# Dilated attention outputs read back into two tiles, and both branches combined behind the fourth and fifth token tile of the next head pair's projection

## The chip, the cores and the metric

One core of one Trainium2 chip runs one program that computes the whole reference. The metric is the time of one execution on the device in microseconds (us); less is better. TensorE (PE in the rows; PEld is its weight load) multiplies matrices, VectorE (DVE), ScalarE (ACT) and GpSimd (POOL) do the element-wise work, and SP issues the DMA transfers. Each engine runs its own queue in order.

## The reference, cut to what matters

A decoder trunk of two layers (an even and an odd one) over 1024 tokens of width 1024, all in float32. The change lies in the even layer's mixer, in the mixture of dilated attention branches with 8 heads of 64. Branches of the same head are joined by a softmax over their log-denominators:

```python
B_BRANCHES = ((128, 1), (512, 4), (2048, 16))

def even_mixer(h, w_in, ...):
    ...
    qh = rms_norm(heads(q), q_g)
    kh = rms_norm(heads(k), k_g)
    vh = heads(vb)
    outs, lses = [], []
    for window, dilation in B_BRANCHES:
        o_r, l_r = dilated_branch(qh, kh, vh, window, dilation)
        outs.append(o_r)
        lses.append(l_r)
    wts = jax.nn.softmax(jnp.stack(lses), axis=0)
    o = jnp.einsum('rbhs,rbhsc->bhsc', wts, jnp.stack(outs))
    ...
    return jnp.concatenate([a_out, b_out], axis=-1) @ w_out
```

The even mixer's other half is a gated MLP over chunks (gMLP), the odd layer is gated linear attention, and each layer ends in a gated feed-forward block.

## The kernel before

The eight heads are worked on in four pairs (`PAIRS`). For each pair p:

- `project(p)` (from line 640) takes the 1024 tokens in eight tiles of 128. For each tile n it does 24 matmuls into `pj` (line 185, called from line 651): queries, keys and values of the pair, against eight cast weight tiles `wq`. Then come the norms of queries and keys (ScalarE line 656, VectorE line 658, GpSimd lines 135 and 136, VectorE line 660, GpSimd line 662), the value tile `vN` (ScalarE line 664; it also frees the `pj` bank), the turned queries and keys (`qT` line 678, `kT` line 682), and one attention step `unit` for the branch of dilation 1.
- `unit` (line 614) makes, for each of two heads, scores on TensorE (line 600), a masked minimum on VectorE (line 605), an exponential on ScalarE (line 607 or 609), a turn on TensorE (line 625), a copy `pT` (line 630 on VectorE for even i, line 628 on ScalarE for odd i) and the product with the values into `po` (line 633). Minima and denominators go into columns 128 to 131 of a tile `ot`, outputs into its first 128.
- `dilated(p)` (line 698) does eight such units for the branches of dilation 4 and 16 at once, in the order of the residues, and stores both halves to device memory, `od`.
- For each half g of the tokens, a tile `on` (one buffer) is read back from `od` in token order (line 744), and `combine(p, g, ...)` (line 715) joins it with the tile `ot` that `project(p)` left: a minimum `cM` (line 720), two subtractions and an exponential `cE` (lines 723 and 724), denominators and a reciprocal `cD` (lines 727 to 729), a factor each (line 730), one multiply on GpSimd and one on VectorE (line 733), the sum (line 735), and a store to `bcat` (line 736).

In the program text the combines of pair p stand between `dilated(p)` and `project(p + 1)`. Behind the fourth pair stand `gmlp`, `u_proj` and the output projection.

Weights are loaded and cast by `load_qkv`: raw tiles of two chunks, each chunk cast into two parts by ScalarE (line 100) and VectorE (line 101). The pool of cast weights holds eight tiles, as many as one pair needs, so a tile for the next pair becomes free when the last token tile of this pair has used it. There are two `pj` banks.

The order on each engine is not the order of the text. A planner at build time puts ready instructions of earlier text first, by its own estimate of times, and gives out the buffers of a pool; the resulting queues are fixed, and the waits between engines are added. `keep_in_program_order(ins)`, which the change calls, ties `ins` in that plan behind the instruction of its engine that was traced just before it.

Of the kernel before, what the change touches and what calls it, by code (L numbers as in the profile page):

```python
# [8 lines left out]
F32 = mybir.dt.float32  # L9
# [4 lines left out]
ALU = mybir.AluOpType  # L14
# [4 lines left out]
P = 128  # L19
# [22 lines left out]
def f32(ap):  # L42
    return ap.bitcast(F32)
# [6 lines left out]
def rows(t, n):  # L50
    return t[n * P : (n + 1) * P, :]
# [3 lines left out]
def trunk(ctx: ExitStack, tc: tile.TileContext, a, out):  # L55
    nc = tc.nc
    V, A, G, T, Q = nc.vector, nc.scalar, nc.gpsimd, nc.tensor, nc.sync
# [116 lines left out]
    def tok(n, k):  # L174
        return [hq[k % 2][n // 4][:, i, k // 2, (n % 4) * P : (n % 4 + 1) * P] for i in range(2)]

    def mm_tok(ps, lhs, rhs, nk):

        for k in range(nk):
            L, R = lhs(k), rhs(k)  # L180
            for i in range(2):
                for o, sl in ps:
                    for ii, jj in PASSES:
                        if ii == i:
                            T.matmul(o, L[i], R[jj][:, sl], start=(k == 0 and (ii, jj) == PASSES[0]),  # L185
                                     stop=(k == nk - 1 and (ii, jj) == PASSES[-1]))
# [317 lines left out]
    def load_qkv(p):  # L504
        return [w for kp in range(4)
                for w in load_w(a["w_qkv"][p, kp], f"wq{p}{kp}", 384, gains=g0[:, 2 * kp : 2 * kp + 2])]
# [54 lines left out]
    def attention(ps, at, av, pq, pq0, par0, wq0, gm_open):  # L561
# [30 lines left out]
        def by4(t):  # L592

            return t.rearrange("p s (m r) -> p s r m", r=4)
# [42 lines left out]
            return (at.tile([P, 4, 132], F32, tag="ot", name="ot" + name, bufs=5),  # L637
                    ps.tile([P, 4, P], F32, tag="po", name="po" + name))

        def project(p, ws=None):  # L640


            ws = ws or load_qkv(p)
            pool = pq if p % 2 else pq0
            qT = pool.tile([P, 2, S], F32R, tag="qT", bufs=1, name=f"qT{p}")
            kT = pool.tile([P, 4, S], F32R, tag="kT", bufs=1, name=f"kT{p}")
            vd = dram.tile([S, P], F32, name=f"vd{p}")
            vN, os = [], []
            for n in range(NT):
                pj = ps.tile([P, 512], F32, tag="pj", name=f"pj{p}{n}")  # L650
                mm_tok([(pj[:, :384], slice(0, 384))], lambda k: tok(n, k),
                       lambda k: ws[k], KD)
                qn = pq.tile([P, 256], F32, tag="qn", bufs=2, name=f"qn{p}{n}")
                heads = lambda t: t.rearrange("p (h c) -> p h c", c=64)
                rn = r0[:, n : n + 1]
                A.activation(qn, pj[:, :256], AF.Square, scale=rn)
                ssq = small.tile([P, 4], F32, tag="ss4", name=f"ss{p}{n}")
                V.reduce_sum(ssq, heads(qn), axis=AX.X)
                r = inv_rms(ssq, 4, 64, f"rq{p}{n}")
                V.scalar_tensor_tensor(heads(qn), heads(pj[:, :256]), rn, r[:, :, None].to_broadcast([P, 4, 64]),  # L660
                                       op0=ALU.mult, op1=ALU.mult)
                G.tensor_tensor(qn, qn, gqk, op=ALU.mult)
                vN.append(pq.tile([P, P], F32, tag="vN", bufs=3, name=f"vN{p}{n}"))
                A.mul(vN[n], pj[:, 256:384], rn)  # L664
                Q.dma_start(rows(vd, n), vN[n])
                qs = pq.tile([P, 2, P], F32R, tag="qs", bufs=2, name=f"qs{p}{n}")
                ks = pq.tile([P, 4, P], F32R, tag="ks", bufs=2, name=f"ks{p}{n}")
                split([qs[:, :, :64], qs[:, :, 64:]], heads(qn[:, :P]), hi=G.tensor_copy)
                kk = ks.rearrange("p (h i) (x c) -> p h i x c", i=2, x=2)
                split([kk[:, :, i] for i in range(2)], heads(qn[:, P:])[:, :, None, :].to_broadcast([P, 2, 2, 64]),  # L670
                      hi=G.tensor_copy)
                tq = ps.tile([P, 2, P], F32R, tag="tq", name=f"tq{p}{n}")
                for j in range(2):
                    T.transpose(tq[:, j, :], qs[:, j, :], identr)
                qN = pq.tile([P, 2, P], F32R, tag="qN", bufs=2, name=f"qN{p}{n}")
                A.copy(qN, f32(tq))
                four = lambda t: t.rearrange("p s (r m) -> p s r m", r=4)[:, :, :, 32 * n : 32 * n + 32]
                V.tensor_copy(four(qT), by4(f32(tq)))
                tk = ps.tile([P, 4, P], F32R, tag="tq", name=f"tk{p}{n}")
                for j in range(4):  # L680
                    T.transpose(tk[:, j, :], ks[:, j, :], identr)
                (V.tensor_copy if n % 2 else A.copy)(four(kT), by4(f32(tk)))

                if n % 4 == 0:
                    ot, po = outputs(f"{p}n{n}")
                    os.append(ot)
                m0 = max(n - 1, 0)
                unit(p, f"{p}n{n}", n % 4, ot, po, lambda s: qN[:, s, :],
                     lambda s, i: kT[:, 2 * s + i, :].rearrange("p (r m) -> p r m", r=4)[:, :, 32 * m0 : 32 * n + 32],
                     vN[m0 : n + 1], (mband, None), lambda t: t.rearrange("p (m r) -> p r m", r=4))  # L690
                if n % 4 == 3:
                    A.copy(ot[:, :, :P], po)
            v4 = av.tile([P, 4, 2, P], F32, tag="v4", name=f"v4{p}", bufs=1)
            for b in range(2):
                Q.dma_start(v4[:, :, b, :], vd.rearrange("(b m r) c -> b m r c", b=2, r=4)[b])
            return os, qT, kT, v4

        def dilated(p, qT, kT, v4):

            od = dram.tile([S, 132], F32, name=f"od{p}")  # L700
            for g in range(2):
                ot, po = outputs(f"{p}d{g}")
                for i in range(4):
                    r, b = 2 * g + i // 2, i % 2
                    at0 = r * 256
                    unit(p, f"{p}d{g}{i}", i, ot, po, lambda s: qT[:, s, at0 + b * P : at0 + b * P + P],
                         lambda s, part: kT[:, 2 * s + part, at0 : at0 + b * P + P],
                         [v4[:, r, j, :] for j in range(b + 1)], (mboth, count))
                A.copy(ot[:, :, :P], po)
                for b in range(2):  # L710
                    Q.dma_start(od.rearrange("(b m r) c -> b m r c", b=2, r=4)[b][:, 2 * g : 2 * g + 2, :],
                                ot.rearrange("p (r b) c -> p r b c", b=2)[:, :, b, :])
            return od

        def combine(p, g, os):

            nm = [o[:, :, 128:130] for o in os]
            den = [o[:, :, 130:132] for o in os]
            M = small.tile([P, 4, 2], F32, tag="cM", bufs=2, name=f"cM{p}{g}")
            V.tensor_tensor(M, nm[0], nm[1], op=ALU.min)  # L720
            e = small.tile([P, 2, 4, 2], F32, tag="cE", bufs=2, name=f"cE{p}{g}")
            for i in range(2):
                V.tensor_sub(e[:, i], M, nm[i])
            A.activation(e, e, AF.Exp)
            dd = small.tile([P, 2, 4, 2], F32, tag="cD", bufs=2, name=f"cD{p}{g}")
            for i in range(2):
                V.tensor_mul(dd[:, i], e[:, i], den[i])
            V.tensor_add(dd[:, 0], dd[:, 0], dd[:, 1])
            V.reciprocal(dd[:, 1], dd[:, 0])
            V.tensor_tensor(e, e, dd[:, 1:2].to_broadcast([P, 2, 4, 2]), op=ALU.mult)  # L730
            for i, eng in ((0, G), (1, V)):
                ov = os[i][:, :, :P].rearrange("p n (s c) -> p n s c", s=2)
                eng.tensor_tensor(ov, ov, e[:, i, :, :, None].to_broadcast([P, 4, 2, 64]), op=ALU.mult)
            o0, o1 = (o[:, :, :P] for o in os)
            V.tensor_add(o0, o0, o1)
            Q.dma_start(bcat[g].rearrange("(n p) c -> p n c", p=P)[:, :, p * P : p * P + P], o0)

        made = project(0, wq0)
        for p in range(PAIRS):
            os, *qkv = made  # L740
            od = dilated(p, *qkv)
            for g in range(2):
                on = at.tile([P, 4, 132], F32, tag="on", name=f"on{p}{g}", bufs=1)
                Q.dma_start(on, od.rearrange("(n p) c -> p n c", p=P)[:, 4 * g : 4 * g + 4, :])
                combine(p, g, [os[g], on])
            if p + 1 < PAIRS:
                made = project(p + 1)
            if p + 2 == PAIRS:
                par0.close()
                gm = gm_open()  # L750
# [315 lines left out]
```

## Time and profile before

| | us |
|---|---|
| median of 3 runs | 2256.8 |
| lowest and highest | 2255.03 and 2261.63 |
| the profiled execution's own time | 2256.71 |
| its span (first to last instruction) | 2255.0 |
| TensorE busy | 2189.3 |
| VectorE busy | 1483.4 |
| ScalarE busy | 998.6 |
| GpSimd busy | 470.0 |

All rows come from the one profiled execution. Times in them count from the start of its span. A stretch is a window of that time; the granted clock is 1.00 at TensorE's upper level (2.4 GHz) and 0.50 at the lower (1.2 GHz), and a value between is a mean over the stretch. An arrow `<-` in square brackets names what ended the idle time of the engine ahead of the instruction. Buffer numbers are left out of tile names, but a pair's number stays in some: `pT1n` belongs to pair 1 and the branch of dilation 1, `pT1d` to its dilated part.

### The profile page before, as it was taken

How to read it: one execution, taken by the hardware profiler on the slowest of the kernel's cores; microseconds unless marked ns; L12 is line 12 of the kernel's file. 1: busy time of each engine (PE TensorE's matmuls, PEld its weight loads, DVE VectorE, ACT ScalarE, POOL GpSimd, SP SyncE). 2: the span in 40 equal slices, each digit the busy share in tenths (PEclk: the TensorE clock that was granted, in tenths of full speed). 3: DMA queues.
4: the chain of work that ended last, by engine and by line, in shares of the span. 5: the costliest groups of instructions: out<-in, count | busy, mean ns of one | idle time of the engine just before them, and what ended most of it. 6: DMA issues, size and time to landing. Idle time of an engine off the chain costs nothing.

```text
span 2255.0 us, 29873 instructions
## 1 busy us (share of the span) xinstructions
PE 2189.3 (97%) x10800; PEld 1857.6 (82%) x10800; DVE 1483.4 (66%) x2414; ACT 998.6 (44%) x1830; POOL 470.0 (21%) x487
## 2 busy tenths in 40 slices
PE   7989999998999999999999999999999999999999
PEld 7988978787888888878889888877788888888887
DVE  5567655548888888855574444234889898986554
ACT  5445446336544444434453333222644444444443
POOL 3333320000424243200010111000134343420000
PEclk9999999999999999999999999999999999999999
DMA  4122221442444444585562111356254444457555
GB/s 138 47 72 61 62 68 43 126 161 75 155 167 155 160 156 165 179 281 184 205 227 75 52 57 52 108 168 203 75 171 159 157 158 155 157 181 275 197 187 205
DMA packets 139540, 320.22 MB, mean 142 GB/s; under 512 B 15952, under 2 KB 40528, under 8 KB 139392
## 3 DMA queue, kind: packets, MB, share of 16 engines
q1 hardware_dynamic: 139392, 318.31, 42.1%
q8 instruction: 85, 1.39, 0.3%
q14 instruction: 63, 0.52, 0.1%
HBM read 223.29 MB, written 94.96 MB: 141 GB/s over the span
## 4 chain that ended last, share of the span: by engine, by line
PE 85%; DVE 5%; DMA 4%; ACT 3%; issue 1%; POOL 1%; SPq 0%; DVEq 0%; ACTq 0%; POOLq 0%
PE pgB L254 11%; PE puB L254 11%; PE po L185 6%; PE puC L254 5%; PE pgC L254 5%; PE pv L185 5%; PE pdB L361 5%; PE pdC L361 5%; PE pj L185 4%; PE pdO L361 4%; PE pr L185 4%; PE puA L254 3%; PE pgA L254 3%; PE pdP L361 2%; PE pdQ L361 2%; PE pk L197 2%
## 5 line engine op out<-in xcount | busy, mean ns | idle before, releaser
L96 DVE TENSOR_TENSOR da<-ar,da 128x512 fp32r<-128x512 f32 x154 | 106.2, 689 | 156.9 <-ACT da L95 156.8
L95 ACT CAST da<-ar 128x512 fp32r<-128x512 f32 x154 | 95.9, 623 | 211.2 <-PE pdC L361 92.3
L185 PE MATMUL po<-wo,hq 128*128 128x512 f32 x768 | 185.0, 395 | 2.3 <-ACT hq L100 1.3
L185 PEld LDWEIGHTS po<-wo,hq 128*128 128x128 f32 x768 | 141.6, 188 | 31.3 <-ACT hq L100 2.3
L185 PE MATMUL pj<-wq,hq 128*128 128x384 f32 x768 | 156.2, 353 | 3.2 <-ACT vN L664 2.1
L185 PE MATMUL pv<-wv,hq 128*128 128x256 f32 (+2 forms) x960 | 154.6, 315 | 0.3 <-ACT vN L664 0.2
L185 PEld LDWEIGHTS pv<-wv,hq 128*128 128x128 f32 x960 | 135.0, 192 | 9.6 <-ACT vN L664 0.4
L185 PEld LDWEIGHTS pj<-wq,hq 128*128 128x128 f32 x768 | 138.4, 198 | 4.6 <-ACT vN L664 3.2
L361 PE MATMUL pdB<-dw,da 128*128 128x512 f32 x528 | 136.2, 391 | 1.2 <-ACT dw L95 1.2
L361 PE MATMUL pdC<-dw,da 128*128 128x512 f32 x528 | 135.8, 390 | 0.0
L361 PEld LDWEIGHTS pdB<-dw,da 128*128 128x128 f32 x528 | 98.7, 188 | 22.5 <-ACT dw L95 1.6
L361 PEld LDWEIGHTS pdC<-dw,da 128*128 128x128 f32 x528 | 99.0, 188 | 20.5
L225 POOL TENSOR_TENSOR S1g<-rg 128x512 f32<-128x512 f32 x20 | 28.3, 1417 | 417.3 <-DMA wsd<-D 212.5
L96 DVE TENSOR_TENSOR dw<-wr,dw 128x512 fp32r<-128x512 f32 x154 | 105.7, 686 | 10.4 <-ACT dw L95 10.0
L135 POOL TENSOR_SCALAR rn<-ssq 128x1 f32<-128x1 f32 x24 | 9.6, 399 | 452.4 <-ACT h L143 245.8
L361 PE MATMUL pdO<-dw,da 128*128 128x512 f32 x396 | 102.2, 389 | 0.1
L95 ACT CAST dw<-wr 128x512 fp32r<-128x512 f32 x154 | 95.0, 617 | 13.4 <-DMA wr<-in_w_dn 7.3
L185 PE MATMUL pr<-wr,hq 128*128 128x512 f32 x384 | 97.9, 404 | 0.0
L361 PEld LDWEIGHTS pdO<-dw,da 128*128 128x128 f32 x396 | 74.3, 188 | 15.9 <-DVE dw L96 0.6
L185 PEld LDWEIGHTS pr<-wr,hq 128*128 128x128 f32 x384 | 71.2, 188 | 14.5
L283 DVE SCALAR_TENSOR_TENSOR t<-g,cw,t 128x1022 f32<-128x1022 f32 x44 | 76.8, 1744 | 0.1
L282 DVE SCALAR_TENSOR_TENSOR t<-g,cw,t 128x1023 f32<-128x1023 f32 x44 | 62.5, 1420 | 15.5 <-ACT t L281 15.5
(910 smaller groups left out, 5207.2 us busy)
## 6 DMA issues: line engine op xcount, KB each, us to landing
ar<-actd SPq DMA_DIRECT2D x70, 512.0 KB, 3.5
rg<-in_w_gate SPq DMA_DIRECT2D x44, 512.0 KB, 3.5
ru<-in_w_up SPq DMA_DIRECT2D x44, 512.0 KB, 4.5
rd<-in_w_down SPq DMA_DIRECT2D x44, 512.0 KB, 3.6
wsd<-D SPq DMA_DIRECT2D x88, 256.0 KB, 2.2
wr<-wsd SPq DMA_DIRECT2D x40, 512.0 KB, 4.3
actd<-t SPq DMA_DIRECT2D x66, 256.0 KB, 2.1
wr<-in_w_dn SPq DMA_DIRECT2D x30, 512.0 KB, 4.9
```

The lines of the kernel that those rows point to most:

```text
L95: (hi or A.copy)(dst[0], src)
L96: (lo or V.tensor_sub)(dst[1], src, f32(dst[0]))
L135: G.tensor_scalar(r, ssq, 1.0 / n, EPS, op0=ALU.mult, op1=ALU.add)
L185: T.matmul(o, L[i], R[jj][:, sl], start=(k == 0 and (ii, jj) == PASSES[0]), stop=(k == nk - 1 and (ii, jj) == PASSES[-1]))
L197: T.matmul(ps[h], L[i], hq[k % 2][h][:, jj, k // 2, :], start=(k == 0 and (ii, jj) == PASSES[0]), stop=(k == KD - 1 and (ii, jj) == PASSES ...
L225: (G if f else V).tensor_tensor(sums[name], x, y, op=op)
L254: T.matmul(o, L[ii][:, j * P : j * P + P], right[p][:, jj, j, :], skip_group_check=more, start=(not more and j == 0 and (ii, jj) == PASSES ...
L282: V.scalar_tensor_tensor(t[:, 1:], g[:, : S - 1], w(1), t[:, 1:], op0=ALU.mult, op1=ALU.add)
L283: V.scalar_tensor_tensor(t[:, 2:], g[:, : S - 2], w(0), t[:, 2:], op0=ALU.mult, op1=ALU.add)
L361: T.matmul(o, L[ii][:, t * P : t * P + P], R[jj], skip_group_check=more, start=start and not more and (ii, jj) == PASSES[0], stop=stop and ...
```

## The change

`on` gets two buffers, and both loads of a pair are issued behind `dilated(p)`, ahead of either combine. The combines move into `project(p + 1)`: half 0 behind the attention step of token tile 3 (the fourth), half 1 behind that of tile 4 (the fifth). For the last pair, which has no next projection, both follow the loads directly. The first VectorE instruction of a combine (line 720 before) is pinned with `keep_in_program_order`.

```diff
--- before.py
+++ after.py
@@ -637,7 +637,7 @@
             return (at.tile([P, 4, 132], F32, tag="ot", name="ot" + name, bufs=5),
                     ps.tile([P, 4, P], F32, tag="po", name="po" + name))
 
-        def project(p, ws=None):
+        def project(p, ws=None, then=None):
 
 
             ws = ws or load_qkv(p)
@@ -690,6 +690,8 @@
                      vN[m0 : n + 1], (mband, None), lambda t: t.rearrange("p (m r) -> p r m", r=4))
                 if n % 4 == 3:
                     A.copy(ot[:, :, :P], po)
+                if then and n in (3, 4):
+                    then(n - 3)
             v4 = av.tile([P, 4, 2, P], F32, tag="v4", name=f"v4{p}", bufs=1)
             for b in range(2):
                 Q.dma_start(v4[:, :, b, :], vd.rearrange("(b m r) c -> b m r c", b=2, r=4)[b])
@@ -717,7 +719,7 @@
             nm = [o[:, :, 128:130] for o in os]
             den = [o[:, :, 130:132] for o in os]
             M = small.tile([P, 4, 2], F32, tag="cM", bufs=2, name=f"cM{p}{g}")
-            V.tensor_tensor(M, nm[0], nm[1], op=ALU.min)
+            tc.keep_in_program_order(V.tensor_tensor(M, nm[0], nm[1], op=ALU.min))
             e = small.tile([P, 2, 4, 2], F32, tag="cE", bufs=2, name=f"cE{p}{g}")
             for i in range(2):
                 V.tensor_sub(e[:, i], M, nm[i])
@@ -739,12 +741,20 @@
         for p in range(PAIRS):
             os, *qkv = made
             od = dilated(p, *qkv)
+            ons = []
             for g in range(2):
-                on = at.tile([P, 4, 132], F32, tag="on", name=f"on{p}{g}", bufs=1)
+                on = at.tile([P, 4, 132], F32, tag="on", name=f"on{p}{g}", bufs=2)
                 Q.dma_start(on, od.rearrange("(n p) c -> p n c", p=P)[:, 4 * g : 4 * g + 4, :])
-                combine(p, g, [os[g], on])
+                ons.append(on)
+
+            def then(g):
+                combine(p, g, [os[g], ons[g]])
+
             if p + 1 < PAIRS:
-                made = project(p + 1)
+                made = project(p + 1, then=then)
+            else:
+                then(0)
+                then(1)
             if p + 2 == PAIRS:
                 par0.close()
                 gm = gm_open()
```

## Rows read from the trace of the kernel before

**Rows 1.** The page: busy time, share of the span and instructions of TensorE.

```profile
...
PE 2189.3 (97%) x10800; PEld 1857.6 (82%) x10800; DVE 1483.4 (66%) x2414; ACT 998.6 (44%) x1830; POOL 470.0 (21%) x487
...
```

**Rows 2.** Busy time by stretch: length, engines with counts, clock, DMA.

```profile
...
62.60:91.40 28.80, 26.41 (x179) 25.28 (x177) 18.06 (x45) 13.88 (x36) 11.84 (x21) 1.00 0.25 71
130.60:169.50 38.90, 31.83 (x185) 30.20 (x183) 22.54 (x60) 14.28 (x41) 14.74 (x22) 0.87 0.28 79
208.80:246.60 37.80, 32.14 (x181) 30.83 (x180) 22.03 (x59) 14.30 (x40) 13.68 (x21) 0.82 0.32 90
286.60:325.50 38.90, 33.61 (x179) 28.98 (x178) 23.99 (x56) 17.66 (x36) 12.31 (x20) 0.96 0.29 80
...
```

**Rows 3.** Waits of TensorE, 92 to 420 us: who for whom, total, times, longest.

```profile
...
PE po1n L633 <- DVE pT1n L630: 4.1, 1, 4.1
PE po2n L633 <- DVE pT2n L630: 3.8, 1, 3.8
PE po3n L633 <- DVE pT3n L630: 3.8, 1, 3.8
...
PE pj L185 <- ACT vN L664: 2.1, 2, 1.1
...
```

**Rows 4.** Groups of TensorE, first stretch: busy, mean ns, idle before, releaser.

```profile
...
L633 PE MATMUL po0n<-vN,pT0n 128*128 128x64 f32 x32 | 4.2, 274 | 1.2 <-DVE pT0n L630 1.0 <-ACT pT0n L628 0.2
...
```

**Rows 5.** VectorE in order of time, second boundary: start, length, instruction, idle before.

```profile
...
126.02 0.10 DVE L605 DVE_READ_ACCUMULATOR2_ANT ot1n<- 128x1 f32 x1
128.21 0.17 DVE L720 TENSOR_TENSOR cM<-ot0n,on 128x8 f32<-128x8 f32 x1 [2.10 <-DMA on<-od]
...
136.13 0.17 DVE L720 TENSOR_TENSOR cM<-ot0n,on 128x8 f32<-128x8 f32 x1 [3.41 <-DMA on<-od]
...
137.15 0.71 DVE L728 TENSOR_TENSOR cD<-cD 128x8 f32<-128x8 f32 x1
...
139.20 0.63 DVE L605 CUSTOM_DVE_ANT_1 sm1n<-sc1n,mband 128x256 f32<-128x256 f32 x1
...
141.25 0.68 DVE L735 TENSOR_TENSOR ot0n<-ot0n,on 128x512 f32<-128x512 f32 x1
...
145.93 0.68 DVE L630 COPY pT1n<-pP1n 128x512 f32<-128x512 f32 x1
...
```

**Rows 6.** ScalarE in order of time, second boundary.

```profile
...
136.61 0.22 ACT L724 ACTIVATE cE<-cE 128x16 f32<-128x16 f32 x1 [5.24 <-DVE cE L723]
...
141.28 1.11 ACT L100 ACTIVATE wq<-wq20r,g 128x384 fp32r<-128x384 f32 x2
...
```

**Rows 7.** SP's queue in order of time, second boundary.

```profile
...
132.91 0.43 SPq L744 DMA_DIRECT2D on<-od  x1
...
```

**Rows 8.** TensorE in order of time, second boundary.

```profile
...
137.47 3.94 PE L185 MATMUL pj<-wq,hq 128*128 128x384 f32 x21 [1.14 <-ACT vN L664]
...
148.66 5.89 PE L185 MATMUL pj<-wq,hq 128*128 128x384 f32 x20
...
```

**Rows 9.** VectorE in order of time, first stretch.

```profile
...
67.62 0.62 DVE L605 CUSTOM_DVE_ANT_1 sm0n<-sc0n,mband 128x256 f32<-128x256 f32 x1
...
69.85 1.15 DVE L101 SCALAR_TENSOR_TENSOR wq<-wq10r,g,wq 128x384 fp32r<-128x384 f32 x2
...
73.38 0.68 DVE L630 COPY pT0n<-pP0n 128x512 f32<-128x512 f32 x1
...
```

**Rows 10.** GpSimd in order of time, second boundary.

```profile
...
137.11 0.73 POOL L662 TENSOR_TENSOR qn<-qn,gqk 128x256 f32<-128x256 f32 x1 [3.02 <-DVE cD L727]
...
138.64 1.55 POOL L733 TENSOR_TENSOR ot0n<-ot0n,cE 128x512 f32<-128x512 f32 x1
...
```

**Rows 11.** The tile `on`: from the issue of its load to landing.

```profile
...
DMA to landing us min/median/max: 2.9/3.2/4.5
```

**Rows 12.** Busy time by stretch, two more stretches.

```profile
...
146.00:168.00 22.00, 19.50 (x103) 18.57 (x104) 11.29 (x30) 5.09 (x16) 5.80 (x11) 0.77 0.26 72
400.00:417.00 17.00, 16.25 (x72) 13.16 (x71) 9.69 (x30) 8.23 (x10) 3.04 (x2) 1.00 0.20 48
...
```

## The prediction

> **What bounds the kernel now.** The page comes first: TensorE is busy for 97% of the span [rows 1], so a change to the small vector work of the attention can only win where TensorE stands still or runs on its lower clock level. I therefore asked next, stretch by stretch, where that happens, and then what ended each idle time.
>
> The table of stretches [rows 2] carries most of the argument. Each of its four stretches begins in the seventh token tile of one projection and reaches into the third tile of the next (the last one reaches into the gMLP's value projection): the place where one pair's weights run out and the next pair's must be cast. The first one has no combine in it, since no pair has been through its dilated branch yet; the other three each hold both combines of the pair before. Stretches 1 to 3 do nearly the same TensorE work (179, 185 and 181 matmuls), yet the first takes 28.8 us and the others 38.9 and 37.8. TensorE's idle time is span minus busy time: 2.39, 7.07, 5.66 and 5.29 us. The granted clock is 1.00 in the first, 0.87, 0.82 and 0.96 in the others: part of each was at 1.2 instead of 2.4 GHz. So the first stretch is a control made by the kernel itself.
>
> The waits of TensorE [rows 3] name the idle time: once per pair 4.1, 3.8 and 3.8 us for a VectorE copy of `pT` (line 630), and twice about 1 us for ScalarE's `vN`. In the control the same copy costs 1.0 us [rows 4].
>
> Why the copy is late is read from the three queues at the second boundary. Engines run in the order that the planner wrote, so a wait holds all that is queued behind it. VectorE finishes tile 3's scores at 126.1, then waits 2.10 us for the first `on` and begins combine 0 at 128.21. Later it waits 3.41 us for the second `on`, begins combine 1 at 136.13, and only at 139.20 does tile 4's scores (line 605); the `pT` of tile 4 follows at 145.93, behind most of the casts [rows 5]. ScalarE's exponential of combine 1 waits 5.24 us in ScalarE's queue, and its casts (line 100) start at 141.28 [rows 6]. The second `on` can't come earlier: one buffer, so its load is issued at 132.91, after combine 0 [rows 7]. TensorE meanwhile starts the pair's last token tile at 137.47 and the next pair's first at 148.66, 11.2 us apart [rows 8]. In the control tile 4's second score step runs at 67.62, VectorE's casts (line 101) from 69.85 and the `pT` at 73.38, with no wait for a DMA among them [rows 9].
>
> **The change, part by part.** The sum is made against the profiled execution, 2256.71 us (span 2255.0), which is 0.1 us below the median of 2256.8.
>
> *Combine 0 behind the fourth tile.* The pin puts its first instruction behind the VectorE instruction traced just before it: tile 3's second line 605. The trace has it exactly there already, at 128.21 behind the 126.02 one [rows 5]. So I expect no move and no gain: the wait of 2.10 us stays, and TensorE has projection matmuls over it. With both loads issued together, `on` 0 may land later; the landings go from 2.9 to 4.5 us around 3.2 [rows 11], so up to 1.3 us more wait per pair. I take zero, as TensorE is not waiting there.
>
> *Second buffer, combine 1 behind the fifth tile.* This moves `min`, the two subtractions, the exponential, four small products, the reciprocal, both multiplies, the sum and the store of combine 1 behind the `pT` copy of tile 4, and its load some 8 us earlier. SP gets the load right behind the first and ahead of the `vd` stores: one issue of 0.4 us, while nothing waits for `vd` until the dilated branch. Four gains follow, each per boundary.
>
> First, `vN` of tile 5 no longer stands behind the exponential: the gap of 1.1 us at the second boundary and the other of 1.0 go [rows 3], **2.1**.
>
> Second, tile 4's scores come as in the control, before the last token tile instead of 1.7 us behind its start [rows 5, 8], and ScalarE's casts follow at once. The `pT` gaps shrink to the control's 1.0: 4.1 + 3.8 + 3.8 - 3 x 1.0 = **8.7**.
>
> Third, the clock. Busy time above the control's 26.41 is 5.42 and 5.73 us; six and two more matmuls at 26.41/179 = 0.15 us explain 0.9 and 0.3; so 4.5 and 5.4 are the lower level's. In the fourth stretch (other shapes) a clock of 0.96 over 38.9 us means 2 x 0.04 x 38.9 = 3.1 us at half rate, at the cost ratio of the two others (9.9 for 2 x (0.13 x 38.9 + 0.18 x 37.8) = 23.7 us) 1.3. Sum 11.2. I take two thirds, **7.5**, because gaps of over 1 us remain and the level may still fall once. The trace shows 0.42 us lost per us at half rate. The Trainium skill ("TensorE: Matmul & The Clock Gate", Terms) counts throttled time times (1 - K/N), one half here; by an estimate from it the whole term is 13.4 and two thirds of it 8.9, and the time 1.4 lower.
>
> Fourth, the price: combine 1 now falls among the casts. From its first instruction to the next scores VectorE takes 3.07 us, and 0.68 for the sum [rows 5]: between 0 (it fits into VectorE's idle time, 10.7 of 28.8 us in the control [rows 2]) and 3.7 us per boundary. Behind `pT` only three of the control's eight casts are left, and the projection takes them one by one, so half of 3.07: **-1.5** each, -4.5. The Trainium skill ("SBUF — State Buffer", Who interferes with whom) says that a VectorE instruction with two SBUF inputs and a reading GpSimd instruction block each other for a whole instruction. The trace agrees: line 728, started while GpSimd ran line 662, took 0.71 us, and line 720 of the same shape 0.17 [rows 5, 10]. If each cast boundary paid the full 1.55 us of a GpSimd multiply, as an estimate by that rule [rows 10], the time would be 4.7 higher.
>
> *The last pair.* Both loads are now ahead of both combines, so the second wait goes. TensorE is busy 16.25 of 17 us there [rows 12]: zero, bounds -0.7 and +0.7.
>
> Sum: 2.1 + 8.7 + 7.5 - 4.5 = 13.8; 2256.7 - 13.8 = **2243**. Bounds: all clock back, combine free, the last pair's 0.7 too: 2256.7 - 22.7 = 2234; no clock back and the full 3.7 each: 2256.7 - 10.8 + 11.1 = 2257.
>
> **Rivals.** *The gap changes its name.* `pT` comes early, but the exponential of combine 1 sits in ScalarE's queue ahead of the casts and waits for `pT`; then the next pair's weights are late by what `pT` was early. For it: TensorE has no other work there, since the weight buffers are freed only by the last tile. Against: in the control the casts start ahead of `pT` [rows 9]. TensorE would then keep its gaps and clock, and only the 2.1 us of `vN` go: 2254.6.
>
> *Slower: combine 1 blocks tile 5.* VectorE's 3.7 us and the GpSimd multiply stand ahead of tile 5's key copy and scores, which the next gap waits for. It decides from the point where tile 5's scores are later than the end of the next pair's first token tile. Each boundary then pays 3.7 more and saves only `vN`: 2256.7 + 11.1 - 2.1 = 2265.7. Against it: VectorE is busy 11.29 of 22 us from 146 to 168 [rows 12], so there is room.
>
> *It doesn't do what it says.* The pin orders one instruction; priorities change for all others, and the planner may order all engines anew so that the gap stands elsewhere. Then 2256.7, with a few us either way.
>
> **How the numbers follow.** Forecast (2234 to 2250): 0.62. Gap renamed: 0.18. Slower: 0.12. No effect: 0.08. The range of 2233 to 2258 leaves out most of the slower case and the tail below full recovery. About 0.3% (6.8 us) is what a measurement of this kernel can tell from no change: faster needs less than 2250, slower more than 2263.5. Faster has the forecast's 0.62 and a little of the last case; slower the third case's larger part and a little of the last; so 0.63, 0.24 and 0.13.
>
> **What would show it.** Right: the load of the second `on` directly behind the first, no VectorE wait for it, tile 4's scores ahead of the start of the pair's last token tile, `pT` gaps near 1 us, last tile to next first tile well under 11.2 us, and the clock at 1.00 through most of the three stretches. Combine 0's wait of some 2 us stays. Wrong: TensorE's gaps as long as before under the name of a cast or of tile 5's scores, or stretches 2 to 4 as long as now.

## The result and the profile after

| | before | after |
|---|---|---|
| median, us | 2256.64 (6 runs) | 2236.39 (6 runs, 2230.64 to 2240.61) |
| ratio, 95% interval | | 0.9907 [0.9885, 0.9928] |
| the profiled execution's own time / span, us | 2256.71 / 2255.0 | 2234.04 / 2232.3 |

The kernel became faster by 0.93%: 20.3 us between the medians, 22.7 between the profiled executions. Forecast were 2243.0, 13.8 us less than before. Measured again in five more rounds (below), the same kernel gave 2237.77 against 2252.99 for the kernel before in the same rounds, 0.9932 [0.9915, 0.9949]: 15.2 us. That median is of five executions; a sixth took 2713.63 us at a mean granted clock of 0.75, a slow state of the chip that is left out.

Busy time by stretch, kernel after, columns as in [rows 2]: length, then PE, PEld, DVE, ACT, POOL busy with their counts, clock, DMA share, GB/s. The difference between the length and PE's busy time is TensorE's idle time. The stretches begin and end at the same token tiles; the last ends at the third tile of the gMLP's value projection. In the kernel before that mark lies at 318.6, so its fourth stretch by these marks is 32.0 us long.

```profile
58.50:87.20 28.70, 26.32 (x178) 25.19 (x176) 18.07 (x45) 13.80 (x36) 11.84 (x21) 1.00 0.25 71
126.50:155.30 28.80, 26.28 (x177) 25.15 (x176) 21.01 (x57) 14.19 (x37) 14.80 (x23) 1.00 0.36 101
194.70:224.40 29.70, 26.62 (x179) 25.37 (x177) 20.75 (x56) 14.28 (x37) 14.88 (x23) 1.00 0.35 107
265.00:294.00 29.00, 26.47 (x155) 23.40 (x153) 19.70 (x48) 16.87 (x34) 12.69 (x19) 1.00 0.37 106
```

The second stretch, which was 38.9 us long [rows 2], now takes 28.8, as long as the control's 28.7 (the first stretch, which holds no combine), though VectorE does 2.9 us and GpSimd 3.0 us more in it. The clock is 1.00 in all four.

VectorE in order of time, kernel after, second boundary: the answer to [rows 5]. Lines 693 to 740 of before are two higher here: line 720 is 722.

```profile
121.81 0.11 DVE L605 DVE_READ_ACCUMULATOR2_ANT ot1n<- 128x1 f32 x1
123.95 0.17 DVE L722 TENSOR_TENSOR cM<-ot0n,on 128x8 f32<-128x8 f32 x1 [2.04 <-DMA on<-od]
...
130.91 0.63 DVE L605 CUSTOM_DVE_ANT_1 sm1n<-sc1n,mband 128x256 f32<-128x256 f32 x1 [0.55 <-PE sc1n L600]
...
133.70 1.15 DVE L101 SCALAR_TENSOR_TENSOR wq<-wq20r,g,wq 128x384 fp32r<-128x384 f32 x2
...
137.23 0.68 DVE L630 COPY pT1n<-pP1n 128x512 f32<-128x512 f32 x1
137.83 0.15 DVE L722 TENSOR_TENSOR cM<-ot0n,on 128x8 f32<-128x8 f32 x1
...
142.93 0.57 DVE L732 TENSOR_TENSOR cE<-cE,cD 128x16 f32<-128x16 f32 x1
143.53 0.69 DVE L735 TENSOR_TENSOR on<-on,cE 128x512 f32<-128x512 f32 x1
144.14 0.61 DVE L605 CUSTOM_DVE_ANT_1 sm1n<-sc1n,mband 128x256 f32<-128x256 f32 x1
```

Combine 0 stands where it stood and waits 2.04 us for its load. Behind it nothing of combine 1 is left: tile 4's scores run at 130.91, the casts follow, the copy `pT` runs at 137.23, and combine 1 starts right behind it, at 137.83, with no wait. The second load was issued together with the first (SP, answer to [rows 7]), and ScalarE's casts start at 133.06, ahead of combine 1's exponential (answer to [rows 6]):

```profile
119.85 1.09 SPq L747 DMA_DIRECT2D on<-od  x2
```

```profile
133.06 1.11 ACT L100 ACTIVATE wq<-wq20r,g 128x384 fp32r<-128x384 f32 x2
...
140.09 0.22 ACT L726 ACTIVATE cE<-cE 128x16 f32<-128x16 f32 x1 [0.84 <-DVE cE L725]
```

TensorE in order of time, kernel after, same boundary (answer to [rows 8]), then its waits from 92 to 420 us (answer to [rows 3]; total, times, longest):

```profile
130.95 4.36 PE L185 MATMUL pj<-wq,hq 128*128 128x384 f32 x24
...
137.96 1.10 PE L633 MATMUL po1n<-vN,pT1n 128*128 128x64 f32 x8 [1.02 <-DVE pT1n L630]
...
139.34 4.40 PE L185 MATMUL pj<-wq,hq 128*128 128x384 f32 x24
```

```profile
PE pm L545 <- DVE mx L546: 2.3, 1, 2.3
PE pP3d L625 <- DVE mv L535: 2.1, 1, 2.1
PE po2n L633 <- DVE pT2n L630: 1.6, 2, 1.0
PE po3n L633 <- DVE pT3n L630: 1.4, 1, 1.4
...
PE po1n L633 <- DVE pT1n L630: 1.0, 1, 1.0
PE pv L185 <- ACT gv L531: 0.9, 2, 0.7
...
PE sc3d L600 <- DVE ot3d L605: 0.7, 1, 0.7
PE po3d L633 <- ACT ot3n L692: 0.5, 1, 0.5
```

The kernel before has one row among its own that counts here (same view):

```profile
PE pP3d L625 <- DVE ot3d L610: 2.6, 3, 1.6
```

The first row of TensorE's order of time holds the end of the seventh token tile and the start of the last one (at 132.01) with no wait for `vN` between them; the next pair's first tile follows at 139.34, 7.3 us later instead of 11.2. The `pT` gaps are 1.0, 1.0 and 1.4. The two longest waits lie behind the fourth pair's projection. That for line 546 is new; that for line 535 stands where the same matmuls waited 2.6 us for line 610 before.

**Where the 22.7 us of the profiled executions lie.** The seventh tile of the first pair, up to which the two kernels do the same work, starts at 62.6 before and at 58.5 after. These 4.1 us are not put down to the change: in the twelve other profiles, none of the kernel before, the same tile starts anywhere between 58.4 and 62.2 us, and TensorE ran at 0.50 for 10.2 us ahead of it in the kernel before (47.5 to 57.7) and for 6.8 in the kernel after (44.1 to 50.9). The second stretch gives 10.1, the third 8.1. From the fourth pair's seventh tile to the first matmul of the output projection's product, the two kernels need the same time:

```profile
sum 141.20, PE 131.42 PEld 110.22 DVE 81.90 ACT 76.33 POOL 20.28; mean PE 131.42 PEld 110.22 DVE 81.90 ACT 76.33 POOL 20.28
```

```profile
sum 141.30, PE 131.48 PEld 109.81 DVE 81.19 ACT 76.73 POOL 21.04; mean PE 131.48 PEld 109.81 DVE 81.19 ACT 76.73 POOL 21.04
```

(sums of 286.6 to 427.8 before, of 265.0 to 406.3 after). What the last boundary gained in idle time, the stage behind it gave back. The rest, 0.5, lies between the stretches and downstream.

### The profile page after: what moved, and what is told of

Same layout as the page of the kernel before. It is cut to its first block, busy times and chain, and to the rows that moved or that the text cites. A ratio compares the mean times of both kernels' runs of the same rounds, so it can differ in the third digit from the quotient of the medians.

```text
span 2232.3 us, 29872 instructions
## 1 busy us (share of the span) xinstructions
PE 2176.2 (97%) x10800; PEld 1845.9 (83%) x10800; DVE 1477.6 (66%) x2414; ACT 998.1 (45%) x1830; POOL 476.2 (21%) x487
## 4 chain that ended last, share of the span: by engine, by line
PE 89%; DVE 4%; ACT 3%; DMA 2%; issue 1%; POOL 0%; SPq 0%; ACTq 0%; DVEq 0%; POOLq 0%
PE puB L254 11%; PE pgB L254 10%; PE po L185 7%; PE pv L185 6%; PE puC L254 5%; PE pgC L254 5%; PE pdB L361 5%; PE pdC L361 5%; PE pj L185 5%; PE pdO L361 4%; PE pr L185 4%; PE pgA L254 3%; PE puA L254 2%; PE pdP L361 2%; PE pdQ L361 2%; PE pk L197 2%
## 5 line engine op out<-in xcount | busy, mean ns | idle before, releaser
L185 PE MATMUL pj<-wq,hq 128*128 128x384 f32 x768 | 148.1, 342 | 1.0 <-ACT wq L100 1.0
L185 PEld LDWEIGHTS pj<-wq,hq 128*128 128x128 f32 x768 | 132.5, 189 | 1.4 <-ACT wq L100 1.4
L282 DVE SCALAR_TENSOR_TENSOR t<-g,cw,t 128x1023 f32<-128x1023 f32 x44 | 60.4, 1374 | 15.3 <-ACT t L281 15.3
```

Source lines behind the costliest of these rows:

```text
L282: V.scalar_tensor_tensor(t[:, 1:], g[:, : S - 1], w(1), t[:, 1:], op0=ALU.mult, op1=ALU.add)
```

## The experiments

**Theory.** What stands in VectorE's queue ahead of tile 4's scores decides, waiting or working: once the scores are late, `pT` is late, and TensorE, with no other work at a boundary, stands still and then loses clock. Behind `pT` the same work is hidden. **Rivals:** the second buffer and the early load alone make the gain (the place doesn't matter); the move in the text is enough and the pin does nothing; combine 1 still costs time at its new place; the combines' absence would give more still.

### The second buffer without the new place, and the new place without the second buffer

The first diff is against the kernel before.

```diff
             od = dilated(p, *qkv)
+            ons = []
             for g in range(2):
-                on = at.tile([P, 4, 132], F32, tag="on", name=f"on{p}{g}", bufs=1)
+                on = at.tile([P, 4, 132], F32, tag="on", name=f"on{p}{g}", bufs=2)
...
-                combine(p, g, [os[g], on])
+                ons.append(on)
+            for g in range(2):
+                combine(p, g, [os[g], ons[g]])
             if p + 1 < PAIRS:
```

> Only the second buffer and the early load of both halves; both combines stay ahead of the next projection in the text, no pin. The queue of VectorE now has both minima one behind the other, ahead of tile 4's scores. Theory A (VectorE's standing still for the second load is what costs): no wait for the second load, stretch 2 (seventh tile of pair 1 to third tile of pair 2) 29 to 32 us, time near 2240. Rival B (combine 1's own 3 us of VectorE ahead of tile 4's scores are enough to open the gap): pT gaps of 3 us or more, stretch 2 over 35 us, time near 2250.

2243.64 us, ratio 0.9962 [0.9948, 0.9976]: between 0.4 of the gain (of 0.9907) and a little over half (of 0.9932). Both expectations are met in part: the stretch is 31.0 us long, and the time lies between the two. VectorE in order of time, second boundary of this kernel:

```profile
125.18 0.17 DVE L720 TENSOR_TENSOR cM<-ot0n,on 128x8 f32<-128x8 f32 x1 [2.22 <-DMA on<-od]
...
125.94 0.17 DVE L720 TENSOR_TENSOR cM<-ot0n,on 128x8 f32<-128x8 f32 x1
...
129.67 2.14 DVE L735 TENSOR_TENSOR ot0n<-ot0n,on 128x512 f32<-128x512 f32 x2
...
133.95 0.60 DVE L605 CUSTOM_DVE_ANT_1 sm1n<-sc1n,mband 128x256 f32<-128x256 f32 x1
```

The second wait is gone, but both combines now stand ahead of tile 4's scores as work. The `pT` gaps are 1.5, 1.5 and 2.0, and a wait of 1.4 us for `vN` is still there at this boundary.

The second diff, like all that follow except that of the kernel without combines, is against the changed kernel.

```diff
...
+            def back(g):
+                on = at.tile([P, 4, 132], F32, tag="on", name=f"on{p}{g}", bufs=1)
...
+            back(0)
+
             def then(g):
                 combine(p, g, [os[g], ons[g]])
+                if g == 0:
+                    back(1)
```

> Combines behind the fourth and fifth tile with one buffer: the second load is issued behind combine 0, as before the change. Theory A: it lands some 5 us before combine 1 is due, so no wait; stretches 2 to 4 as in the changed kernel (28.8, 29.7, 28.7 us), time 2234 to 2239. Rival (the second buffer is needed): a wait of 1 us or more at combine 1 and a time of 2242 or more.

2234.25, 0.9916 [0.9891, 0.9941], stretches 28.9, 29.6 and 30.7: the whole gain with one buffer. At the new place the second buffer adds nothing that can be measured; at the old place it gives about half. Behind the fifth tile combine 1 finds its load landed at the three boundaries.

### Without the pin

```diff
-            tc.keep_in_program_order(V.tensor_tensor(M, nm[0], nm[1], op=ALU.min))
+            V.tensor_tensor(M, nm[0], nm[1], op=ALU.min)
```

> The changed kernel without the pin. Its VectorE queue has both minima again one behind the other ahead of tile 4's scores, as with the second buffer alone. Theory A (only the place of combine 1 in VectorE's queue matters, not its place in the text): stretches as with the second buffer alone (31.0, 32.0, 31.5 us instead of 28.8, 29.7, 29.0 to the same matmuls), time 0.4% to 0.5% above the changed kernel's. Rival (the move in the text is enough, the pin does nothing): stretches and time of the changed kernel.

2241.09, 0.9955 [0.9937, 0.9974]: the same as two buffers without the move. The planner puts combine 1 back behind combine 0 (its `cM` at 126.92, 0.8 us behind the first), and tile 4's scores come at 134.91. Moving the text did nothing here without the tie. The pin alone, at the old place, was not run.

### How much work, and where

```diff
             Q.dma_start(bcat[g].rearrange("(n p) c -> p n c", p=P)[:, :, p * P : p * P + P], o0)
+            if g == 1 and p + 1 < PAIRS:
+                for _ in range(4):
+                    V.tensor_add(o1, o1, o1)
```

> The changed kernel with four more VectorE additions of 128x512 (2.8 us) behind the sum of combine 1, for the first three pairs; the output doesn't use them. Theory A (VectorE has room behind the casts): stretches 2 to 4 grow by less than 0.5 us each, time as the changed kernel's. Rival (every VectorE instruction at the boundary is on the path): 2.8 us more per stretch, time 8 us above.

The other two kernels have the same adds behind combine 0's sum (`g == 0`), four and nine of them.

> The same four additions behind the sum of combine 0, which puts 2.8 us of work ahead of tile 4's scores with no DMA wait; all else in VectorE's queue stays. Theory A (what stands ahead of tile 4's scores counts, wait or work, beyond some 1.5 us of slack): the pT gap grows from 1.0 to about 2 us and the stretches by 1 to 3 us, as with the second buffer alone; time 3 to 8 us above the changed kernel's. Rival (the place doesn't matter): as the run with the additions behind combine 1.

> Nine additions (6.2 us) in that place: as much as the kernel before had there with its wait of 3.4 us and combine 1's 3.1 us. Theory A: the gaps come back in full, pT 4 us, stretches 37 to 39 us, the clock below 0.9 in two of them, and the time of the kernel before within 4 us. Rival (the wait for the DMA did something that work doesn't, or the planner's order was the cause): stretches under 34 us.

Four adds (2.8 us) behind combine 1: 2232.46, 0.9926 [0.9902, 0.995], nothing lost; stretches 29.0, 31.4 (with 192 matmuls instead of 179) and 28.5 at a clock of 1.00, and in them 2.5, 3.1 and 2.7 us of idle time, where the changed kernel has 2.5, 3.1 and 2.5. The total says less than these: the planner's order of this kernel happens to lack the wait for line 546 behind the fourth pair, 2.3 us in the changed kernel. The same four behind combine 0: 2241.29, 0.9958 [0.9944, 0.9972], stretches 32.3, 33.2 and 29.3 with 4.2, 3.5 and 2.8 us of idle time and clocks of 0.95, 0.90 and 1.00. Nine there: 2251.98, 1.0004 [0.9991, 1.0017], the time of the kernel before, although no combine 1 and no second wait stand ahead of the scores. Its first two stretches with a combine come near the expected 37 to 39 us, the last does not (33.9). The three stretches, and its waits of TensorE for `pT`:

```profile
128.30:165.20 36.90, 30.42 (x182) 28.68 (x182) 27.54 (x69) 14.46 (x41) 16.95 (x22) 0.91 0.27 79
204.60:241.40 36.80, 32.09 (x191) 30.76 (x189) 26.95 (x70) 15.52 (x43) 15.77 (x21) 0.86 0.28 87
282.00:315.90 33.90, 30.14 (x163) 26.85 (x161) 29.99 (x69) 16.30 (x38) 15.33 (x19) 0.90 0.29 86
```

```profile
PE po1n L633 <- DVE pT1n L630: 3.6, 1, 3.6
PE po2n L633 <- DVE pT2n L630: 3.0, 1, 3.0
```

Read across the kernels at the second boundary, the start of tile 4's first line 605, counted from the start of the stretch, orders them:

| kernel | tile 4's scores, us into the stretch | `pT` gap, us | TensorE idle in the stretch, us |
|---|---|---|---|
| control (first stretch of after) | 4.4 | 1.0 | 2.4 |
| after; one buffer; fifth and sixth; no combines; four adds behind | 4.4 | 1.0 | 2.4 to 2.8 |
| no pin | 6.0 | 1.5 | 3.8 |
| four adds ahead | 6.3 | 1.5 | 4.2 |
| two buffers, not moved | 6.5 | 1.5 | 4.2 |
| nine adds ahead | 8.0 | 3.6 | 6.5 |
| before | 8.6 | 4.1 | 7.1 |

The stretches of the three rows in the middle, in the table's order:

```profile
128.90:161.00 32.10, 28.32 (x177) 26.69 (x177) 22.06 (x50) 13.55 (x36) 14.55 (x24) 0.95 0.31 90
129.70:162.00 32.30, 28.11 (x177) 26.67 (x176) 24.02 (x61) 13.92 (x37) 15.83 (x23) 0.95 0.31 90
127.50:158.50 31.00, 26.76 (x178) 25.11 (x176) 22.55 (x50) 13.75 (x36) 15.04 (x24) 1.00 0.32 94
```

Idle time grows with the lateness from the start, by 0.9 to 1.2 us per us: 1.6 us late costs 1.4, 2.0 late 1.9, 3.6 late 4.1 and 4.1 late 4.7. The `pT` gap alone hides that, because up to 1.4 us stand under another name, the wait for `vN` (0.9, 1.2, 1.4, 1.1 and 1.1 us in the last five rows). At the third boundary the idle time follows the lateness as well (nine adds: scores at 5.9 us, 1.6 us more idle than after; before: 6.9 and 2.6), but the gaps of this table don't carry over: scores at 5.9 us go with a `pT` gap of 3.0 there. No difference shows between VectorE waiting and VectorE working.

### Combine 0 moved too

```diff
-                if then and n in (3, 4):
-                    then(n - 3)
+                if then and n in (4, 5):
+                    then(n - 4)
```

> The changed kernel with the combines behind the fifth and sixth tile, so that combine 0 no longer waits 2.0 us for its load. Theory A: TensorE has projection matmuls over that wait, so nothing is gained, 2234 to 2239. Rival (every wait of VectorE in the attention delays the scores): the three pairs gain 1 to 2 us each, 2230 to 2233. If combine 1 now meets tile 5's key copy and scores: slower, 2240 or more.

2235.82, 0.9922 [0.9897, 0.9947]; combine 0 now starts at 141.33 without a wait, and the stretches are 29.1, 29.7 and 29.1. Combine 0's wait of 2 us was under TensorE's cover, as forecast.

### No combines at all

```diff
-                combine(p, g, [os[g], on])
+                Q.dma_start(bcat[g].rearrange("(n p) c -> p n c", p=P)[:, :, p * P : p * P + P], os[g][:, :, :P])
```

> The kernel before without any combine: the output of the first branch is stored as it is, and the dilated output is stored but not read back, so the second branch's share is missing. Theory A: with nothing ahead of tile 4's scores each stretch becomes the control's, 28.8 us, and the time that of the changed kernel, 2232 to 2238: the changed kernel's combines cost nothing. Rival (the combines still cost their VectorE time where they now stand, 1.5 us each): 2228 to 2231.

A miss: 2247.04, 0.9973 [0.9959, 0.9988], slower than the changed kernel, which does more. (This diff is against the kernel before.) The gaps were as expected, 1.0, 1.0 and 1.5. But the clock fell, even in its first stretch, the control, where no kernel has a combine; first to third stretch:

```profile
60.90:91.10 30.20, 27.82 (x178) 26.70 (x176) 18.04 (x45) 13.84 (x36) 11.87 (x21) 0.94 0.26 77
130.40:162.40 32.00, 29.60 (x178) 28.31 (x177) 18.32 (x45) 13.86 (x36) 11.98 (x22) 0.89 0.26 73
201.70:234.30 32.60, 29.63 (x178) 28.40 (x176) 17.89 (x45) 13.91 (x36) 12.80 (x22) 0.90 0.28 87
```

The idle time is what answers the rival: 2.4, 3.0 and 2.6 us in the three stretches behind the control, and 2.5, 3.1 and 2.5 in the changed kernel. At their new place the combines cost TensorE about 0.1 us per boundary, if anything.

Up to the output projection the profiled execution, the longest of its ten (2251.9), is still 15.3 us ahead of before; of these 10.5 are lost again behind it. The queues there stand in the changed kernel's order but for some twenty instructions, and the granted clock fell for less time than in the changed kernel, yet the 3696 matmuls of line 254 took 1453.8 us in place of 1443.8. Why was not settled. The total of a kernel with less work is thus no bound; its stretches can be compared.

### The changed kernel once more

> The changed kernel once more, on the chip of the two runs beside it: 0.990 to 0.993 of the kernel before. A second profile shows whether its clock at the three boundaries stays at the upper level (1.00 in all three stretches) or falls now and then.

2237.77, 0.9932 [0.9915, 0.9949]. The gaps are those of the first profile to 0.03 us (1.04 and 1.17, 1.02 and 1.17 at the two boundaries), yet the clock isn't:

```profile
126.30:158.10 31.80, 29.26 (x178) 28.20 (x176) 21.48 (x57) 14.24 (x37) 15.15 (x23) 0.89 0.30 92
197.50:230.30 32.80, 29.70 (x179) 28.45 (x177) 20.79 (x56) 14.23 (x37) 14.86 (x23) 0.90 0.33 97
```

Each stretch is 3 us longer at the same queue order, the same matmuls and the same idle time (2.5 and 3.1 us). In the first of them the lower level was granted from 146.6 to 153.5 us, just behind the second gap, which ended at 145.4; in the first profile the same gap was followed by 1.00. The chip is not the reason: the first kernel under *The last pair* has, in these two stretches, the same instructions in the same order on every engine, was run on the chip of this repeat, and kept 1.00 in both (28.8 and 29.6 us). The first of them:

```profile
128.90:157.70 28.80, 26.28 (x177) 25.15 (x176) 21.18 (x57) 14.20 (x37) 15.02 (x23) 1.00 0.35 101
```

Part of the gain thus comes or doesn't from one execution to the next, and 2230 to 2241 us is one kernel.

### The last pair

In the kernel after, VectorE stands 3.51 us for the last pair's load, and TensorE's mixing matmuls wait for the bias addition (line 546) queued behind. VectorE, then TensorE, kernel after:

```profile
374.55 0.17 DVE L722 TENSOR_TENSOR cM<-ot3n,on 128x8 f32<-128x8 f32 x1 [3.51 <-DMA on<-od]
```

```profile
376.17 1.16 PE L545 MATMUL pm<-mx,ws 128*128 128x256 f32 x4 [2.28 <-DVE mx L546]
```

Three kernels move these two combines into `u_proj`, the gMLP's second projection, behind its sixth and seventh tile (the second of them with the fifth and sixth tile for the other pairs as well), then behind its third and fourth:

```diff
             V.tensor_mul(mixed[n], mixed[n], t)
+            if n in (5, 6):
+                then(n - 5)
...
-            else:
-                then(0)
-                then(1)
```

> The changed kernel with the last pair's combines behind the sixth and seventh tile of the gMLP's second projection. In the changed kernel VectorE waits 3.5 us for the last pair's load, pinned behind its dilated branch, with the gMLP's bias step in the queue behind it; TensorE stands 2.3 us for that, and its clock falls for 3.4 us. Theory A (the same disease as at the other boundaries): that gap goes, 2 to 4 us less than the changed kernel. Rival (the output projection now waits for the late combine): a gap at its first tiles, no gain or slower.

> Both together: combines behind the fifth and sixth tile, the last pair's behind the gMLP's second projection. Theory A: the waits of combine 0 cost nothing, so the time is that of the run with the last pair alone moved, within 2 us. Rival: 2 to 4 us less than that.

2245.7, 0.9969 [0.9954, 0.9984], and 2247.71, 0.9977 [0.9965, 0.9988]: the rival of the first expectation. The wait at 376 went, and another came; TensorE in order of time, first of the two kernels:

```profile
416.18 1.11 PE L405 MATMUL pc<-ident,cat 128*128 128x128 f32 x4 [11.28 <-DMA cat<-bcat]
```

The output projection reads `bcat`, whose last store now goes out at 412.41. With the third and fourth tile it is early enough:

> The changed kernel with one edit: the last pair's two combines stand behind the third and fourth tile of the gMLP's second projection (u_proj), between the place that the change gave them (directly behind the loads) and the place of e9 (sixth and seventh tile). Theory (VectorE must not stand still for the last pair's load ahead of the mixing's bias adds, and the output projection must not wait for the combine's store): both gaps of TensorE are gone, that of 2.3 us at the mixing matmuls (changed kernel, 373.9 us) and that of 11.3 us at the output projection's first transposes (e9), so from the second projection's first matmul to the output projection 61 to 63 us against 64.2 in the changed kernel, and a median 1 to 4 us under the changed kernel's, 2232 to 2237, if the planner's order downstream is as good. Rival 1 (any move of the last pair's combines makes the store late): a gap of over 3 us under the name of the cat load at about 405 us, time 2240 to 2248. Rival 2 (the planner's new order downstream costs more than the gap): no gap at either place and yet a stage or a rest of the program longer by 3 us or more, time 2238 to 2245.

2233.88, 0.9912 [0.9894, 0.9931]. Both waits are gone; from the second projection's first matmul to the output projection it is 347.3 to 409.1, 61.8 us, against 64.2 (63.2 in the changed kernel's repeat). From the fourth pair's seventh tile to the output projection, 271.7 to 409.1:

```profile
sum 137.40, PE 128.86 PEld 107.43 DVE 81.36 ACT 76.77 POOL 20.80; mean PE 128.86 PEld 107.43 DVE 81.36 ACT 76.77 POOL 20.80
```

This is 3.9 us less than after, 1.3 of it idle time and 2.6 busy time at the same work, which is clock. The clock's part is not the move's: the changed kernel's repeat has the same busy time between the same marks, and 1.4 us more idle time:

```profile
270.90:409.70 138.80, 128.86 (x669) 107.39 (x667) 81.05 (x222) 76.73 (x121) 20.68 (x35) 1.00 0.22 66
```

So the move is worth some 1.4 us here. In its second and third stretch the clock fell as in the repeated run (0.89 and 0.90); in the time of the whole program it can't be told from the changed kernel.

The pin is not what put the combines ahead of most bias additions. In the kernel with two buffers and no pin, and in the one without the pin, VectorE stands 3.0 and 3.1 us there, and TensorE waits 2.0 us in each:

```profile
382.49 0.17 DVE L720 TENSOR_TENSOR cM<-ot3n,on 128x8 f32<-128x8 f32 x1 [3.01 <-DMA on<-od]
```

```profile
385.09 0.17 DVE L722 TENSOR_TENSOR cM<-ot3n,on 128x8 f32<-128x8 f32 x1 [3.08 <-DMA on<-od]
```

## Why the prediction was right, point by point

The direction, the mechanism and the range held. The gain was 20.3 us at first and 15.2 when repeated, where 13.8 were forecast. That the second figure is so near is in part luck: the price of combine 1 and the last pair were both mis-sized, in opposite directions, and the clock moved by 6 us between two profiles of one kernel.

| term, us | forecast | measured in the first profile |
|---|---|---|
| combine 0's wait | 0 | 0 (2.04 us of wait stay; moved away, nothing changes) |
| `vN` gaps | 2.1 | 2.1 |
| `pT` gaps | 8.7 | 8.2 (11.7 to 1.02 + 1.03 + 1.44) |
| clock, second and third boundary | 6.6 of 9.9 | 9.6; 3.5 in the repeated profile |
| price of combine 1 | -1.5 per boundary | 0 (idle time within 0.1 of the kernel without combines) |
| of all these, the last boundary and the last pair, netted | 3.2 | -0.1; 2.4 in the repeated profile, all of it clock |
| ahead of the first boundary | 0 | 4.1, not the change's |

- **`vN` and `pT`.** Right in size and for the reason given: scores ahead of the last token tile, load issued with the first, no wait for it. The sizes came from the control stretch, and the changed stretches went to it.
- **The clock.** "I take two thirds" turned out to lie between two outcomes of one kernel. Its reason, that gaps over 1 us remain and the level may still fall, is what the repeat shows; its size was a guess. In the first profile all of it came back: busy time in the two stretches was 26.28 and 26.62, where the control has 26.32. In the repeated one it was 29.26 and 29.70 against 26.30, 6.4 us of 9.9 still lost. The rate held: in the repeated run's second stretch 2 x 0.11 x 31.8 = 7.0 us at half rate cost 2.96, 0.42 per us. The Trainium skill's one half per us ("TensorE: Matmul & The Clock Gate", Terms) is again above what the rows show.
- **The price of combine 1** is the step that failed on size: 1.5 taken between 0 and 3.7, measured 0. The argument was that three casts are left behind `pT` and that combine 1 would delay them by half its time. Three are left, but combine 1's pieces stand between and behind them in VectorE's queue: the last cast starts 13.25 us into the stretch in the control and 13.51 with combine 1, and the next pair's first tile runs without a wait. The last cast, control and second boundary:

```profile
71.72 0.61 DVE L101 SCALAR_TENSOR_TENSOR wq<-wq13r,g,wq 128x384 fp32r<-128x384 f32 x1
...
139.97 0.61 DVE L101 SCALAR_TENSOR_TENSOR wq<-wq23r,g,wq 128x384 fp32r<-128x384 f32 x1
```

Four adds more, 2.8 us, are free in the stretches as well. The lower bound, idle time of VectorE, was the right row. The Trainium skill's rule for VectorE and GpSimd ("SBUF — State Buffer", Who interferes with whom) shows here as line 732, 0.57 us at 142.93 while GpSimd ran line 662, against 0.17 in combine 0; it costs the stretch nothing, so the estimate of 4.7 us by it didn't arise.

- **The last pair** is the other step that failed. "Both loads are now ahead of both combines, so the second wait goes" held, but I looked only at where the combines had been (400 to 417 us). The new order has them at 374.55, directly behind the dilated branch, where a bias addition for the mixing matmuls is due every 2 us or so. Between the fourth pair's seventh tile and the output projection TensorE's idle time is 9.8 us before, 9.8 after and 9.9 in the repeat: the 3.4 us that the boundary saved (`pT` 2.4, `vN` 1.0) came back as the wait for line 546 (2.3) and three small ones (lines 531, 605 and 692, 2.1 together). Moving the two combines behind the third and fourth tile of `u_proj` took 1.3 to 1.4 us of it back.
- **The rivals.** *The gap changes its name* did not happen at the boundaries: the exponential stands behind the casts in ScalarE's queue. It did happen in the last pair, where I had not priced it. *Combine 1 blocks tile 5* did not: tile 5's scores at 144.14 stand ahead of the sum, 17.7 us into the stretch (17.5 in the control), and there is room for 2.8 us more. *It doesn't do what it says* comes nearest in the kernel without the pin, where the planner put combine 1 back: 0.9955.

Open: what decides, at equal gaps, whether the clock falls in one execution and not in the next; and which part of the planner's new order puts the last pair's combines ahead of most bias additions, which it does with and without the pin but not in the kernel with four adds behind.

## What to carry to other kernels

When one boundary of a loop lacks the suspected work, take it as the control and size the gain by it; then ask what stands in the in-order queue ahead of the instruction that the boundary waits for, not how long that work is: here 2.8 us were free behind the copy, and ahead of the scores they cost up to 1.7 us of idle time at a boundary. (The medians of the two kernels lie 9 us apart; the rest is clock and, behind the fourth pair, another order.) Add up idle time under all its names: a gap that doesn't grow may have a neighbour that does. Look where the moved work lands in the last iteration, which has no next one to hide in. A move under a planner needs the tie as well as the new place in the text.

## What the runs showed of the hardware that was not expected

TensorE's clock is not a function of the gaps alone. With two gaps of 1.0 and 1.2 us at a boundary it was at 1.00 in one profile of a kernel and at 0.89 and 0.90 over the stretch in another profile of the same kernel, and again at 1.00 on the second profile's chip in a kernel with the same queues there; in the kernel without combines it fell to 0.94 even in the control, whose idle time is the usual 2.4 us. Each such fall costs 3 us in a stretch of 29 (1.5 in that control), as much as the difference between many of the kernels here, so that a change of a few us is read from the gaps and the stretches rather than from the total.
